# Stores through GpSimd's queue as single packets, and two tokens dealt to other engines

## The chip, the cores and the metric

The kernel runs on one core of a Trainium2 chip. The time is the device time of one execution in microseconds, as the median of several runs; the profile is one execution recorded by the hardware profiler. Its span, from the first to the last instruction, is a little shorter than the device time.

## What is computed

Each of 8 x 256 tokens has a row of 512 numbers and 8 gate weights, one per expert. The weights of a token are divided by their sum, and the row is written out eight times, each time multiplied by one of the eight normalised weights:

```
gate_weights = gate_weights / (np.sum(gate_weights, axis=-1, keepdims=True) + 1e-8)
output = x[:, :, None, :] * gate_weights[:, :, :, None]
```

All is float32. The inputs hold 4.26 MB, the output 33.55 MB: one multiplication per number written, and eight times as much written as read.

## The kernel before

The 2048 tokens are laid over 128 partitions, 16 tokens to a partition, so that what lies in one partition is contiguous in the output too. "Token j" below means the j-th token of every partition, so one step over j makes 128 x 8 x 512 numbers, 16 KB in each partition.

The inputs come in by four loads. The gates and the first two tokens (`HEAD`) are issued ahead of the barrier at the program's entry, from SyncE's and ScalarE's queue; tokens 2 to 12 (the body) and 13 to 15 follow on SyncE's queue (L72, L75). Lines 80 to 83 normalise all gates at once on VectorE.

The output is built in `ring`, which has ten slots of one token each. The list `CHUNKS` has five entries (first token, number of tokens, first slot): stores one to five write 2, 3, 3, 4 and 4 tokens. Stores four and five use slots again: tokens 8 and 9 take the slots 0 and 1 of store one, tokens 10 and 11 the slots 2 and 3 of store two, tokens 12 and 13 the slots 6 and 7 of store three; tokens 14 and 15 take the slots 8 and 9, which are new. A token that takes a used slot can't be computed before that slot's store has landed.

There are two ways to compute a token. `scale_one` makes one of its eight parts, on ScalarE (L90, an ACTIVATE) or on VectorE (L92, a TENSOR_SCALAR). `scale_token` makes all eight in one VectorE instruction (L95, a TENSOR_TENSOR). Before the change tokens 0, 1 and 3 are shared between both engines; token 2 and the first tokens of stores three, four and five (5, 8 and 12) are ScalarE's; all others, tokens 4 and 9 among them, are VectorE's by L95. The framework puts the instructions of each engine into an order of its own planning and adds the waits on semaphores; the order that results on VectorE for L95 is 4, 6, 7, 9, two tokens of the new slots, 10, 11, 13.

The stores are issued at L120, all on SyncE's queue, one after the other. Store one has an added dependency on the body load, so that it doesn't run among the loads. At the end (L157 of the launch) SyncE waits for all DMAs, and a barrier ends the program. GpSimd does nothing but set four constants at the start.

Of the kernel before, what the change touches and what calls it, by code (L numbers as in the profile page):

```python
# [1 line left out]

# [4 lines left out]

SLOTS = 10
HEAD = 2
TAIL = 13  # L10
CHUNKS = ((0, 2, 0), (2, 3, 2), (5, 3, 5), (8, 4, 0), (12, 4, 6))


def issue_before_entry_barrier(nc, loads):
    names = [bi.ins.name for bi in loads]

    def move(nc):
        blocks = nc.main_func.blocks
        entry = blocks[0].instructions
        moved = []  # L20
        for block in blocks[1:]:
            for ins in list(block.instructions):
                if ins.name in names:
                    block.instructions.remove(ins)
                    moved.append(ins)
        assert sorted(i.name for i in moved) == sorted(names)
        for ins in moved:
            at = next(k for k, other in enumerate(entry) if other.engine == ins.engine)
            entry.insert(at, ins)

    nc.at_finalize(move)


@with_exitstack
def kernel(
    ctx: ExitStack,
    tc: tile.TileContext,
    x: bass.AP,
    gate_weights: bass.AP,
    out: bass.AP,  # L40
):
    nc = tc.nc
    P = 128

    B, S, D = x.shape
    E = gate_weights.shape[-1]
    J = B * S // P

    fp32 = mybir.dt.float32
    mult = mybir.AluOpType.mult  # L50

    x_v = x.flatten_outer_dims().rearrange("(p j) d -> p j d", p=P)
    g_v = gate_weights.flatten_outer_dims().rearrange("(p j) e -> p j e", p=P)
    out_v = out.rearrange("b s e d -> (b s) e d").rearrange(
        "(p j) e d -> p j e d", p=P
    )

    pool = ctx.enter_context(tc.tile_pool(name="pool", bufs=1))

    g_all = pool.tile([P, J, E], fp32)  # L60
    x_all = pool.tile([P, J, D], fp32)
    ring = pool.tile([P, SLOTS, E, D], fp32)
    gsum = pool.tile([P, J, 1], fp32)
    gn = pool.tile([P, J, E], fp32)
    warm = pool.tile([P, 1], fp32)

    first_loads = [
        nc.sync.dma_start(out=g_all, in_=g_v),
        nc.scalar.dma_start(out=x_all[:, 0:HEAD, :], in_=x_v[:, 0:HEAD, :]),
    ]  # L70
    issue_before_entry_barrier(nc, first_loads)
    body_load = nc.sync.dma_start(  # L72
        out=x_all[:, HEAD:TAIL, :], in_=x_v[:, HEAD:TAIL, :]
    )
    nc.sync.dma_start(out=x_all[:, TAIL:J, :], in_=x_v[:, TAIL:J, :])  # L75

    nc.vector.memset(warm, 0.0)  # L77
    nc.scalar.copy(out=warm, in_=warm)  # L78

    nc.vector.reduce_sum(out=gsum, in_=g_all, axis=mybir.AxisListType.X)  # L80
    nc.vector.tensor_scalar_add(out=gsum, in0=gsum, scalar1=1e-8)  # L81
    nc.vector.reciprocal(out=gsum, in_=gsum)  # L82
    nc.vector.tensor_tensor(  # L83
        out=gn, in0=g_all, in1=gsum.to_broadcast([P, J, E]), op=mult
    )

    def scale_one(engine, j, e, slot):
        o_ap, s_ap = ring[:, slot, e, :], gn[:, j, e : e + 1]
        if engine is nc.scalar:
            nc.scalar.mul(out=o_ap, in_=x_all[:, j, :], mul=s_ap)  # L90
        else:
            nc.vector.tensor_scalar_mul(out=o_ap, in0=x_all[:, j, :], scalar1=s_ap)  # L92

    def scale_token(j, slot):
        nc.vector.tensor_tensor(  # L95
            out=ring[:, slot, :, :],
            in0=x_all[:, j : j + 1, :].to_broadcast([P, E, D]),
            in1=gn[:, j, :].unsqueeze(2).to_broadcast([P, E, D]),
            op=mult,
        )  # L100

    for j0, m, s0 in CHUNKS:
        for i in range(m):
            j, slot = j0 + i, s0 + i
            if j < 2:
                for e in range(E):
                    on_act = e < 3
                    scale_one(nc.scalar if on_act else nc.vector, j, e, slot)
            elif j == 2:
                for e in range(E):  # L110
                    scale_one(nc.scalar, j, e, slot)
            elif j == 3:
                for e in range(E):
                    scale_one(nc.scalar if e < 2 else nc.vector, j, e, slot)
            elif i == 0:
                for e in range(E):
                    scale_one(nc.scalar, j, e, slot)
            else:
                scale_token(j, slot)
        store = nc.sync.dma_start(  # L120
            out=out_v[:, j0 : j0 + m, :, :], in_=ring[:, s0 : s0 + m, :, :]
        )
        if j0 == 0:
            tc.add_manual_dep(
                store.ins,
                body_load.ins.name,
                mybir.DependencyInfo(
                    mybir.DependencyClass.Sync, mybir.DependencyReason.DATA
                ),
                reason="no store among the loads",  # L130
            )


# [1 line left out]
_INS = ['x', 'gate_weights']  # L135
_OUTS = [((8, 256, 8, 512), 'float32')]


# [23 lines left out]
```

## Time and profile before

The time before is 92.58 us, the median of 3 runs (92.5 to 92.65). The profiled span is 90.7 us.

| what | value | how to read it |
|---|---|---|
| DMA | 37.81 MB, 417 GB/s over the span | all 16 DMA engines of the core together |
| VectorE busy | 46.7 us of 90.7 | 9 TENSOR_TENSOR of 4420 ns, 16 TENSOR_SCALAR of 482 ns |
| ScalarE busy | 26.4 us | 40 ACTIVATE of 708 ns; overlapping, so eight take 5.0 us |
| GpSimd busy | 0.2 us | four MEMSETs |
| SyncE's final wait for DMA | 33.1 us | from the fifth store's issue to its landing |

In the profile, "SPq L120" is the issue of a store by SyncE's sequencer; the time to landing is counted from there to the moment at which its semaphore is complete. "A <- B" in the list of waits says that A waited for B, with the sum, the number of times and the longest.

### The profile page before, as it was taken

To read this page: it belongs to the slowest core of one execution; us is meant where nothing else is said; L and a number is where in the kernel's file an instruction comes from. 1 tells how busy PE (TensorE), PEld (TensorE's weight loads), DVE (VectorE), ACT (ScalarE), POOL (GpSimd) and SP (SyncE) were. 2 spreads that over 40 slices of the span, in tenths; PEclk is the share of its full clock that TensorE was granted. 3 is DMA by queue.
4 is the path that set the end of the run, shared out by engine and by line. 5 is a ranking of instruction groups with operands and counts; after the bars stand their busy time and mean duration, and the time that the engine had idled before them with its cause. 6 is when DMAs were issued, how large, how long until landed. Compare 5 with 4: busy or idle time off the path is not lost.

```text
span 90.7 us, 140 instructions
## 1 busy us (share of the span) xinstructions
DVE 46.7 (52%) x30; ACT 26.4 (29%) x42; POOL 0.2 (0%) x4
## 2 busy tenths in 40 slices
DVE  0795399999999999999990495000000000000000
ACT  5393399997990000000000497000000000000000
POOL 0000000000000000000000000000000000000000
DMA  4998999999898889888988999999999982999990
GB/s 110 468 467 378 383 536 463 463 390 419 347 694 347 347 347 694 347 347 347 694 347 347 463 463 463 463 463 463 463 463 463 463 347 116 463 463 463 463 463 0
DMA packets 1296, 37.81 MB, mean 417 GB/s; under 512 B 144, under 2 KB 272, under 8 KB 528
## 3 DMA queue, kind: packets, MB, share of 16 engines
q1 hardware_dynamic: 1152, 37.29, 95.5%
q10 hardware_dynamic: 144, 0.52, 1.6%
HBM read 4.26 MB, written 33.55 MB: 417 GB/s over the span
## 4 chain that ended last, share of the span: by engine, by line
DMA 38%; DVE 17%; ACT 5%; ACTq 1%; issue 0%; SPq 0%
DMA out_dram<-ring 28%; DVE ring L95 14%; DMA x_all<-in_x_dram 11%; ACT ring L90 5%; DVE ring L92 3%; ACTq L157 1%; ACTq L90 0%; SPq L120 0%
## 5 line engine op out<-in xcount | busy, mean ns | idle before, releaser
L95 DVE TENSOR_TENSOR ring<-x_all,gn 128x4096 f32<-128x4096 f32 x9 | 39.2, 4420 | 3.5 <-DMA out_dram<-ring 3.5
L90 ACT ACTIVATE ring<-x_all,gn 128x512 f32<-128x512 f32 x40 | 24.9, 708 | 28.8 <-DMA out_dram<-ring 24.5
L92 DVE TENSOR_SCALAR ring<-x_all,gn 128x512 f32<-128x512 f32 x16 | 6.5, 482 | 2.8 <-DMA x_all<-in_x_dram 2.8
L78 ACT ACT_TABLE_LOAD x1 | 1.3, 1283 | 0.9 <-PEq L146 0.9
L80 DVE TENSOR_REDUCE gsum<-g_all 128x16 f32<-128x128 f32 x1 | 0.3, 286 | 1.6 <-DMA g_all<-in_gate_weights_dram 1.6
L77 DVE MEMSET warm<- 128x1 f32 x1 | 0.1, 59 | 1.0 <-PEq L146 1.0
L83 DVE TENSOR_TENSOR gn<-g_all,gsum 128x128 f32<-128x128 f32 x1 | 0.3, 291 | 0.0
L82 DVE RECIPROCAL gsum<-gsum 128x16 f32<-128x16 f32 x1 | 0.3, 252 | 0.0
L78 ACT COPY warm<-warm 128x1 f32<-128x1 f32 x1 | 0.2, 191 | 0.0
L81 DVE TENSOR_SCALAR gsum<-gsum 128x16 f32<-128x16 f32 x1 | 0.2, 176 | 0.0
L146 POOL MEMSET const-bfloat16-1.0<- 128x1 bf16 x1 | 0.1, 102 | 0.0
L146 POOL MEMSET const-uint8-127<- 128x1 uint8 x1 | 0.1, 102 | 0.0
L146 POOL MEMSET const-float32-0.0<- 128x1 f32 x1 | 0.1, 99 | 0.2 <-issue 0.2
L146 POOL MEMSET const-float32-1.0<- 128x1 f32 x1 | 0.1, 99 | 0.0
## 6 DMA issues: line engine op xcount, KB each, us to landing
out_dram<-ring SPq DMA_DIRECT2D x2, 6144.0 KB, 22.1
out_dram<-ring SPq DMA_DIRECT2D x1, 4096.0 KB, 11.5
x_all<-in_x_dram SPq DMA_DIRECT2D x1, 2816.0 KB, 9.6
x_all<-in_x_dram SPq DMA_DIRECT2D x1, 768.0 KB, 11.1
x_all<-in_x_dram ACTq DMA_DIRECT2D x1, 512.0 KB, 3.7
g_all<-in_gate_weights_dram SPq DMA_DIRECT2D x1, 64.0 KB, 2.6
out_dram<-ring SPq DMA_DIRECT2D x2, 28.1
```

What stands on the lines that cost most here:

```text
L77: nc.vector.memset(warm, 0.0)
L78: nc.scalar.copy(out=warm, in_=warm)
L80: nc.vector.reduce_sum(out=gsum, in_=g_all, axis=mybir.AxisListType.X)
L81: nc.vector.tensor_scalar_add(out=gsum, in0=gsum, scalar1=1e-8)
L82: nc.vector.reciprocal(out=gsum, in_=gsum)
L83: nc.vector.tensor_tensor(out=gn, in0=g_all, in1=gsum.to_broadcast([P, J, E]), op=mult)
L90: nc.scalar.mul(out=o_ap, in_=x_all[:, j, :], mul=s_ap)
L92: nc.vector.tensor_scalar_mul(out=o_ap, in0=x_all[:, j, :], scalar1=s_ap)
L95: nc.vector.tensor_tensor(out=ring[:, slot, :, :], in0=x_all[:, j : j + 1, :].to_broadcast([P, E, D]), in1=gn[:, j, :].unsqueeze(2).to_bro ...
L146: nc = _bacc.Bacc("TRN2", target_bir_lowering=False, num_devices=1)
L157: with _tile.TileContext(nc) as tc:
```

## The change

The first store stays on SyncE's queue. Stores two to five are issued by GpSimd instead, whose queue holds nothing else. The flag `single_packet` asks that all of a store's descriptors on one DMA engine form one packet.

Besides, token 4, the last of store two, is made by eight TENSOR_SCALARs of VectorE (L92) in place of one TENSOR_TENSOR (L95); and token 9, the second of store four, goes from VectorE to eight ACTIVATEs of ScalarE (L90). Both are there to let stores two and four be issued earlier.

```diff
+SOFT_FROM = 2
 CHUNKS = ((0, 2, 0), (2, 3, 2), (5, 3, 5), (8, 4, 0), (12, 4, 6))
...
-            elif i == 0:
+            elif j == 4:
+                for e in range(E):
+                    scale_one(nc.vector, j, e, slot)
+            elif i == 0 or j == 9:
                 for e in range(E):
                     scale_one(nc.scalar, j, e, slot)
             else:
                 scale_token(j, slot)
-        store = nc.sync.dma_start(
-            out=out_v[:, j0 : j0 + m, :, :], in_=ring[:, s0 : s0 + m, :, :]
-        )
+        out_ap, in_ap = out_v[:, j0 : j0 + m, :, :], ring[:, s0 : s0 + m, :, :]
+        if j0 < SOFT_FROM:
+            store = nc.sync.dma_start(out=out_ap, in_=in_ap)
+        else:
+            nc.gpsimd.dma_start(out=out_ap, in_=in_ap, single_packet=True)
```

## The prediction

> **What bounds the kernel now.** I read the busy rows of the page first, then the DMA row, then the moments at which the five stores were issued and landed, and last the waits.
>
> ```profile
> span 90.7 us, 140 instructions
> DVE 46.7 (52%) x30; ACT 26.4 (29%) x42; POOL 0.2 (0%) x4
> DMA  4998999999898889888988999999999982999990
> DMA packets 1296, 37.81 MB, mean 417 GB/s; under 512 B 144, under 2 KB 272, under 8 KB 528
> q1 hardware_dynamic: 1152, 37.29, 95.5%
> ```
>
> No compute engine is busy for much more than half of the span, and the DMA row is 8 or 9 in nearly every slice from the second on (the lone 2 stands beside an 8 and is how whole 2.4 us packets fall into 2.27 us slices). One queue holds the 16 engines for 95.5% of the span. The next question is whether the stores ever run out of queued work.
>
> ```profile
> 10.60 45.91 SPq L120 DMA_DIRECT2D out_dram<-ring  x5
> 17.41 0.34 SPq L120 DMA_DIRECT2D out_dram<-ring  x1
> 26.08 0.33 SPq L120 DMA_DIRECT2D out_dram<-ring  x1
> 47.76 0.33 SPq L120 DMA_DIRECT2D out_dram<-ring  x1
> 56.18 0.33 SPq L120 DMA_DIRECT2D out_dram<-ring  x1
> ```
>
> These are the issues (start, length) of stores one to five; the times to landing of that line are 11.5, 19.1, 25.0, 22.7 and 33.6 us. Sums: they land at 22.1, 36.5, 51.1, 70.5 and 89.8. The distances are 14.4, 14.6, 19.4 and 19.3 us for 6.29, 6.29, 8.39 and 8.39 MB: 437, 431, 432 and 435 GB/s, with no hole at any boundary. Each store is issued long before its predecessor lands: ahead by 4.7, 10.4, 3.3 and 14.3 us. That margin is what the change can use up.
>
> ```profile
> ACT ring L90 <- DMA out_dram<-ring: 24.5, 2, 24.0
> DVE ring L95 <- DMA out_dram<-ring: 3.5, 1, 3.5
> SPq L157 <- DMA out_dram<-ring: 33.1, 1, 33.1
> ```
>
> The compute engines wait for the stores to free ring slots, and the end of the program waits 33.1 us for the last store. So the time is the head (first bytes at 1.0 us, the loads, store one behind them), then 67.7 us of stores two to five at 434 GB/s, then about 0.9 us from the last landing to the end of the span. The profile's chain turns to DVE before the third store, because a slot there was released late; with a full DMA row and 10.4 us of margin that part bounds nothing.
>
> **What the Trainium skill says.** "DMA: Bandwidth & Descriptors", section "Issuing engines are not separate DMA queues": a DMA issued from GpSimd runs on the same 16 engines as one from SyncE, so a new queue brings no bandwidth. The trace of before agrees as far as it goes: its two queues (q1 and q10) together never pass the rate of one. Same page, "Queues, rings and completion order": an engine takes turns between queues packet by packet. Here a later store shares the engines with store one. In the records of before, two body-load packets of 22,528 B on q1 took 1202 and 1180 ns where 836 is usual, a delay of two whole 4096 B packets (159 ns each) of q10 and a little more; an engine thus seems to stay with a queue for more than one record. "SBUF — State Buffer", "Who interferes with whom": descriptors for GpSimd's DMAs are written through a port pair that VectorE can lock; `tensor_scalar` in its two-port modes locks it, `tensor_tensor` takes only the read interface and is inferred not to stop descriptors. No GpSimd DMA is in the trace of before, so it can't say.
>
> **The change part by part.**
> *Token 4 from one `TENSOR_TENSOR` to eight `TENSOR_SCALAR`.* Removed: 4420 ns. Added: 8 at the pace of the six before it (2.47 us for six, 0.41 each), 3.3 us. VectorE then ends token 4 at 12.92 + 3.3 = 16.2 instead of 17.3. ScalarE's share of store two (tokens 2 and 3, ten instructions at 11.14/18 = 0.62 us from 10.53) ends at 16.7. So store two becomes ready at 16.7 instead of 17.4, and ScalarE is then what it waits for: 0.7 us more margin. These two-port instructions end before GpSimd can start on its first store, so they can't lock it.
> *Token 9 from VectorE to ScalarE.* VectorE loses 4.42 us between tokens 7 and the next; ScalarE gains 8 x 0.62 = 5.0 us right after token 8 (22.15 to 27.16), done at 32.2 in a stretch in which it waits 24.0 us. Tokens 6 and 7 follow token 4: done at 20.6 and 25.0, so store three is ready at 25.0 instead of 26.0. The two tokens that use fresh slots end at 33.7; tokens 10 and 11 need slots of store two, which lands at 36.5, so VectorE waits about 2.8 us there and ends at 36.5 + 2 x 4.4 = 45.3 instead of 47.7. Store four gains 2.4 us of margin. Tokens 12 and 13 wait for store three at 51.1 as now, 5.0 us: store five ready at 56.2, unchanged.
> *Issue on GpSimd.* Removed: four issues of 0.33 us on SyncE, which nobody waits for. Added: four waits and four descriptor jobs on GpSimd. Nothing else is queued there: its four MEMSETs end at 0.4 us. Price: on SyncE the first load's bytes flow 1.0 us after its issue; the skill's "Latency and other measured facts" gives about 1 us to the first byte for GpSimd and 0.6 for SyncE. I take 1.5 us, low end 1.0; as the high end the case in which descriptors wait for the `TENSOR_TENSOR` that is running, 4.4 + 1.0 = 5.4 us. Margins after the edits, to the landing of the store before: 22.1 - 16.7 = 5.4, 11.5, 51.1 - 45.3 = 5.8 and 14.3 us. Even the high end just fits. On the path: 0.
> *One packet per engine.* Each store has 8 rows per engine (128 over 16). In the packet records a 49,152 B row starts every 1812 ns and a 65,536 B row every 2414 ns. The slope is 602 ns per 16,384 B, 27.2 GB/s per engine, and what is left per row is about 6 ns. If one packet removes it for seven of eight rows: 4 x 7 x 6 = 0.17 us at most; if these gaps belong to rows and not to packets, 0. I take half, 0.08 us.
> *Two queues at once.* Store two is queued from about 18 us while store one has some 3.5 us left. Total bytes are the same; only the order could change.
> Sum: 0 - 0.08 us, so 92.5; I say 92.45, since the earlier readiness also leaves nothing to collide with.
>
> **The rivals.**
> *Faster: the row gaps do vanish, and the handover between stores with them.* 92.58 - 0.17, and with the 4 B record of 9 ns at each store's end some 0.2: 92.35. For it: nothing but the row gaps can still be saved, and they are there. Against it: it is hardly more than the bound of 0.2%.
> *Slower: the software queue runs a little under the hardware queue's rate.* The engines must fetch their descriptors from the memory that GpSimd wrote. "SBUF — State Buffer", "The DMA setup-cost knee", has 425 GB/s for 16 MiB where here 434 is measured. 29.36 MB at 425 take 69.1 us instead of 67.7: +1.4, 94.0 as the far end, 93.2 in the middle. Against it: only eight rows of 48 or 64 KB per engine and store, with time to fetch each next one.
> *Slower: descriptors starved.* If back-to-back `TENSOR_TENSOR`s lock GpSimd until VectorE first pauses (33.7 us), the stream stops from 22.1 to 34.7: +12.6, 105. If the lock passes between two of them, 16.7 + 5.4 = 22.1, nothing lost. For it only the shared port; against it the section above.
> *Slower: store two overtakes store one.* If an engine changes queues after every row of store one, the single packet (14.5 us) cuts in at about 19 us, with two rows of 1.2 us left; one follows at 34, the other behind store three at about 50. Tokens 8 and 9 wait for those slots, ScalarE then needs 10.0 us, and with 1.5 for the issue the queue is empty for about 11 us: 104. Against it: the records of two queues above. With only one row left it lands at about 35 and costs nothing (35 + 10 = 45, as VectorE).
>
> **How the numbers follow.** No change within 0.2% (92.39 to 92.77): 0.36, and the forecast lies in it. Faster: 0.34, of which most is 92.2 to 92.39 and a tenth of all lies further down, for fixed costs outside the span (92.58 - 90.7 = 1.9 us) that I can't see. Slower by a little (a lower rate, a late first descriptor): 0.18, at 92.8 to 94.0. Starved: 0.06. Overtaken: 0.06. The range runs from 91.9 to 94.0: it leaves out the last two cases and a few of a hundred at the low end. Faster 0.34, same 0.36, slower 0.30.
>
> **What would show it.** Right: the DMA row still 8 to 9 through to the end; landings of stores still 14.5 and 19.4 us apart; VectorE waiting some 3 us for the second store, and the fourth issue at about 45; the last wait still the longest. The packet term shows in those distances: shorter by 0.04 us each if the gaps go, longer by 0.3 to 0.4 at 425 GB/s. Starvation would show as a 0 in the DMA row after 22 us with GpSimd's issue long done or stretched; overtaking as a first store that lands after the second, ScalarE's token 8 late, and a hole near 52 us. The prediction is wrong if any wait of GpSimd lies behind something I don't see, if its first store costs over 5.4 us, or if the end of the program has to wait for GpSimd beyond the last landing.

## The result and the profile after

The changed kernel takes 93.85 us (median of 4 runs, 93.59 to 94.09) where the kernel before takes 92.62 (4 runs, 92.5 to 92.78) beside it: 1.0132 times as long, interval 1.0100 to 1.0163. Executions more than 1.5% above the fastest of their kernel are left out of all ratios and intervals, and kept in the medians. Two later comparisons on other chips gave 1.0076 (1.0047 to 1.0105) and 1.0090 (1.0055 to 1.0126). So the change makes the kernel slower, by 0.7 to 1.2 us.

The page of the changed kernel: span, the DMA row in 40 slices, GpSimd's queue (packets, MB, share of the 16 engines), and the body load's time from issue to landing.

```profile
span 91.9 us, 153 instructions
DMA  4999899699799779977997999999999998589990
q0 software_dynamic: 576, 29.36, 74.2%
x_all<-in_x_dram SPq DMA_DIRECT2D x1, 2816.0 KB, 10.4
```

The DMA row has no hole after store one begins: GpSimd's queue is fed in time. But the body load lands after 10.4 us, where the profile of before has 9.6 (the line below), and everything behind it is late by as much. That alone is 0.8 of the 1.2 us between these two spans, and it lies ahead of the first instruction that the change touches.

```profile
x_all<-in_x_dram SPq DMA_DIRECT2D x1, 2816.0 KB, 9.6
```

The order of time, the lines of GpSimd's issues and of VectorE's two tokens of store four (start, length; idle time ahead of it and its releaser):

```profile
17.89 0.67 POOL L128 DMA_DIRECT2D out_dram<-ring  x1 [17.45 <-ACT ring L91]
26.22 0.53 POOL L128 DMA_DIRECT2D out_dram<-ring  x1 [7.67 <-ACT ring L91]
37.45 8.76 DVE L96 TENSOR_TENSOR ring<-x_all,gn 128x4096 f32<-128x4096 f32 x2 [3.14 <-DMA out_dram<-ring]
46.77 0.53 POOL L128 DMA_DIRECT2D out_dram<-ring  x1 [20.02 <-DVE ring L96]
57.34 0.53 POOL L128 DMA_DIRECT2D out_dram<-ring  x1 [10.04 <-ACT ring L91]
```

Less the 0.8 us of the late head, the plan of the compute engines is as predicted: VectorE waits 3.1 us for store two (2.8 predicted), and store four is ready at 45.4 (45.3). Store one lands at 22.85; the landings that follow, at 37.4, 51.95, 71.4 and 90.8, are 14.5, 14.6, 19.5 and 19.3 us apart: within 0.1 us of before. What is new must be sought in tenths of a microsecond: in the head, in those distances, at the end, and outside the span.

Which wait ended last changed in one point. SyncE's waits in the changed kernel:

```profile
SPq L163 <- DMA out_dram<-ring: 79.0, 1, 79.0
```

Before, this line had 33.1 us: SyncE worked off the first waits of its final list while the stores ran, and then waited for store five. Now it waits from 11.8 us on, so the very first wait of the list is the one for the last store, and all others are worked off behind it.

### The profile page after: what moved, and what is told of

Same layout as the page of the kernel before. It is cut to its first block, busy times and chain, and to the rows that moved or that the text cites. A ratio compares the mean times of both kernels' runs of the same rounds, so it can differ in the third digit from the quotient of the medians.

```text
span 91.9 us, 153 instructions
## 1 busy us (share of the span) xinstructions
DVE 41.3 (45%) x36; ACT 31.3 (34%) x50; POOL 2.5 (3%) x8
## 4 chain that ended last, share of the span: by engine, by line
DMA 52%; DVE 5%; ACT 3%; issue 1%; POOLq 1%; SPq 0%; DVEq 0%; ACTq 0%
DMA out_dram<-ring 40%; DMA x_all<-in_x_dram 11%; DVE ring L96 5%; ACT ring L91 3%; POOLq L163 1%; SPq L126 0%; DVEq L96 0%; POOLq L128 0%; ACTq L91 0%
## 5 line engine op out<-in xcount | busy, mean ns | idle before, releaser
L91 ACT ACTIVATE ring<-x_all,gn 128x512 f32<-128x512 f32 x48 | 29.8, 708 | 24.8 <-DMA out_dram<-ring 19.7
L96 DVE TENSOR_TENSOR ring<-x_all,gn 128x4096 f32<-128x4096 f32 x7 | 30.6, 4420 | 9.0 <-DMA out_dram<-ring 9.0
L93 DVE TENSOR_SCALAR ring<-x_all,gn 128x512 f32<-128x512 f32 x24 | 9.7, 481 | 4.0 <-DMA x_all<-in_x_dram 4.0
L128 POOL DMA_DIRECT2D out_dram<-ring x4 | 2.3, 565 | 55.2 <-ACT ring L91 35.2
L78 DVE MEMSET warm<- 128x1 f32 x1 | 0.1, 59 | 1.0 <-PEq L152 1.0
## 6 DMA issues: line engine op xcount, KB each, us to landing
x_all<-in_x_dram SPq DMA_DIRECT2D x1, 2816.0 KB, 10.4
x_all<-in_x_dram SPq DMA_DIRECT2D x1, 768.0 KB, 11.8
```

Source lines behind the costliest of these rows:

```text
L96: nc.vector.tensor_tensor(out=ring[:, slot, :, :], in0=x_all[:, j : j + 1, :].to_broadcast([P, E, D]), in1=gn[:, j, :].unsqueeze(2).to_bro ...
L128: nc.gpsimd.dma_start(out=out_ap, in_=in_ap, single_packet=True)
```

## The experiments

Each ran with the kernel before beside it on the same chip. "Outside the span" is the device time less the recorded span, as a mean over a kernel's runs.

**The parts alone.** Dealing alone (in `after`: `SOFT_FROM = 16`, so all stores stay on SyncE):

> Tokens 4 and 9 dealt as in the changed kernel, but all five stores on SyncE's queue. Theory A (the loss belongs to GpSimd's queue): as before, 92.6 within 0.2, the fourth store ready some 2 us earlier and nothing gained from it. Theory B (the loss belongs to the new dealing, which moves what VectorE and ScalarE do beside the loads): 93.8, with the body load landing at 11.3 us instead of 10.5.

GpSimd's queue alone:

```diff
-            elif j == 4:
-                for e in range(E):
-                    scale_one(nc.vector, j, e, slot)
-            elif i == 0 or j == 9:
+            elif i == 0:
```

> Stores two to five on GpSimd's queue as single packets, tokens 4 and 9 where they were before. Theory A: 93.8 to 94.0, as the changed kernel, since the margins of 3 us and more still hide the issue. Theory B: 92.6. Should the longer issue on GpSimd eat the margin of the fourth store (3.3 us before), a hole would show near 51 us and the time would be above 94.

The last store alone through GpSimd (`SOFT_FROM = 12`):

> Dealt as in the changed kernel, only the fifth store through GpSimd as a single packet. If the loss is one of each store (slower packets), a quarter to a third of it: 92.9 to 93.0. If it is a fixed price of a program that uses GpSimd's queue at all (head and end), 93.6 to 93.9. If it is the head of the chip run alone and not the change, 92.6.

And the changed kernel again:

> The changed kernel once more, for a second profile and a comparison on the chip of the runs beside it. 93.8. If the late body load of its first profile (11.3 us, one packet of 1949 ns) was chance, it is back at about 10.5 here and the time at 93; if it belongs to the change, it is late again.

Measured: dealing alone 92.87, ratio 1.0032 (1.0006 to 1.0058); queue alone 93.62, 1.0071 (1.0035 to 1.0107); last store alone 93.07, 1.0033 (1.0005 to 1.0060); the changed kernel 93.46, 1.0076. The kernel before: 92.67. Neither theory holds alone: both parts seem to cost something, though the first by an amount near what can be told. Single runs of most kernels, of before too, spread from their best by over 1 us.

The queue-alone kernel also gives the price of an issue on GpSimd, because there the margin of store four is as small as before. Its issue of store four:

```profile
48.48 0.53 POOL L125 DMA_DIRECT2D out_dram<-ring  x1 [21.13 <-DVE ring L96]
```

The wait ahead of it ends at 47.96, and the first record of store four is at 50.77, 2.8 us later. Store three's last rows end between 50.70 and 51.08, and, in order of time, the rows of store four start 0.06 us behind them on average and at most 0.12, where in the profiles of before and of the changed kernel it is 0.003. A margin of 3.1 us from the ready moment is thus just used up by GpSimd; the new dealing is needed to hide it. The 2.8 us are an upper value for the issue alone, since the engines were at work on store three until then.

**Presence, framing, and the kernel before as a control.**

> The kernel before, unchanged, run as if it were an experiment: its ratio to itself shows what a comparison can tell, and it gives a second profile of before. Theory C (the head is chance: in every kernel one engine's load packet may stall by 0.5 to 2 us, and store one waits for the slowest engine): body load's end scatters here too, between 10.2 and 12 us, ratio 1.00 within 0.3%. Rival (the head is slower only in the changed kernels): body load again at 10.5 and the time at 92.5.

Without the flag:

```diff
-            nc.gpsimd.dma_start(out=out_ap, in_=in_ap, single_packet=True)
+            nc.gpsimd.dma_start(out=out_ap, in_=in_ap)
```

> The changed kernel without single_packet. If the packets' framing costs (or saves) time, the distance of the last stores' landings changes from 19.4 us and the total moves against 93.5; if framing is without effect, as I now think, 93.4 to 93.6 as the changed kernel, store packets of 1820 and 2425 ns. If store two shares the engines with the rest of store one, row by row, store one lands late, near 25 us, and nothing else moves.

The flag on SyncE's queue, in the kernel before (`single_packet=j0 > 0` at L120):

> The kernel before with single_packet on stores two to five, still on SyncE's queue. If the 6 ns between rows go with one packet per engine: 92.4, packets pitched at 1806 and 2408 ns. If they belong to rows: 92.6, pitches 1812 and 2414. If the framing itself is what makes the changed kernel slower: above 93.

A tiny DMA on GpSimd's queue in the kernel before (`nc.gpsimd.dma_start(out=spare, in_=warm)` after L78):

> The kernel before, plus one DMA of 4 bytes in each partition (SBUF to SBUF) on GpSimd's queue near the start; all stores on SyncE's. If the loss is a fixed price of GpSimd's queue being used at all (end of the program, 0.2 us from the last packet to the end, and the head): 92.8 to 93.3. If it grows with what goes through the queue: 92.6 to 92.7, with the end at 1.2 us as before.

Measured: before against itself 92.64, ratio 0.9983 (0.9962 to 1.0004); without the flag 93.17, 1.0061 (1.0034 to 1.0089); the flag on SyncE 92.69, 0.9990 (0.9959 to 1.0021); the tiny DMA 92.80, 1.0006 (0.9980 to 1.0032). So framing brings nothing on either queue. GpSimd's queue costs little by its presence, at most 0.3 us by this interval; the profile of the tiny DMA has 1.31 us from the last packet to the end of the span where before has 1.19 to 1.22. (This DMA, issued at 2.69 us among the loads, has its first record at 6.60, 3.9 us later.) The control shows how far a comparison can be trusted: 0.2%. Its body load landed after 9.7 us, those of the others between 9.5 and 10.8, and after 11.7 in the second profile of the changed kernel. Dealing alone had 10.8 with all its stores on SyncE, and the changed kernel without the flag 9.6: a late head needs no store on GpSimd, and such a store doesn't always bring it. In the records of such a late head there are one or two 22,528 B rows of 1.4 to 2.4 us in place of 0.84, and store one waits for the slowest engine.

**The stores without the scatter.** To see tenths, three kernels leave out the loads and all arithmetic:

```diff
+    for slot in range(4):
+        nc.vector.memset(ring[:, slot, :, :], 1.0)
...
+        out_ap, in_ap = out_v[:, j0 : j0 + m, :, :], ring[:, 0:m, :, :]
```

> Stores alone: the loads and all arithmetic are left out, the ring is set to 1.0 and the same five stores go out, all on SyncE's queue. No load can stall, so runs should agree within 0.2 us; the output is 1.0 everywhere. About 77.5 us of stores behind a head of 4 to 6 us: 83 to 86.

> The same stores alone (no loads, no arithmetic, the output 1.0 everywhere), stores two to five through GpSimd as single packets. Against the same on SyncE: +0.3 to +0.45 us, if it is the end (0.2) and the four slow rows (0.15). If GpSimd's queue has a lower rate: +1 and more, in all rows. If the greater loss of the changed kernel comes from the loads: less than 0.2. Store two is issued while store one is in full flow: if a single packet cuts in between rows of store one, store one lands after store two.

> As the run before it (no loads, no arithmetic, the output 1.0 everywhere), without single_packet. If framing is without effect: the same time within 0.1 us and the same order of rows. If engines take turns row by row without the flag, rows of stores one and two alternate here and not with the flag.

Measured: 91.02 on SyncE, 91.32 through GpSimd as single packets, 91.32 without the flag, each within 0.02 us over six runs. The pages of the first two, with store one's line:

```profile
span 89.2 us, 53 instructions
q1 hardware_dynamic: 720, 33.55, 87.2%
out_dram<-ring SPq DMA_DIRECT2D x1, 4096.0 KB, 11.2
```

```profile
span 89.6 us, 53 instructions
q0 software_dynamic: 576, 29.36, 76.0%
out_dram<-ring SPq DMA_DIRECT2D x1, 4096.0 KB, 13.2
```

GpSimd's queue costs 0.30 us, fifteen times the scatter, and the flag 0.00. (My 83 to 86 us left out that the four memsets come one by one, so that store one starts at 9.4 us; the differences don't hang on it.) The packet records show where: the mean over the 16 engines of each engine's n-th row, in ns.

```
                         rows of store one (32,768 B)                 store two (49,152 B)
all on SyncE             1219 1250 1218 1231 1228 1222 1214 1232      1834 1820 1820 1820 ...
GpSimd, single packets   1219 1248 1218 1220 1250 1295 1223 1219      1914 1832 1821 1820 ...
GpSimd, no flag          1219 1248 1218 1220 1248 1299 1223 1220      1914 1833 1822 1820 ...
```

GpSimd issues at 13.99 to 15.18 and 18.25 to 19.30. The fifth and sixth row of store one (15.2 to 17.8 us) and the first two of store two (20.2 to 24) follow these issues, and together they are 187 ns longer than on SyncE; all later rows are equal within 3 ns. The rate of the queue is thus not lower; rows that are under way after an issue take longer. By what means, no record shows. The other 0.1 us is at the end: from the last packet to the end of the span 1.27 us instead of 1.15.

Store two does not overtake store one here. It is issued with half of store one still to go, yet store one's rows end at 20.32 (on SyncE 20.23), in their usual order, flag or no flag. But store two's first row comes at 20.24, some 6.2 us after the issue, when store one has no row left, so that rows of the two never compete. Only store one's landing is 2.0 us later, 13.2 for 11.2: the 4 B records that complete its semaphore come at 22.06 to 22.25, behind the first row of store two.

The last store back on SyncE (`if j0 < SOFT_FROM or j0 == 12`):

> The changed kernel with the fifth store back on SyncE's queue, stores two to four on GpSimd's. The theory has two terms: (1) at the end, SyncE's list of final waits begins with the semaphore of the last GpSimd store, so that the waits for long finished DMAs are worked off behind it, 0.06 us each; (2) rows in transfer while GpSimd issues a store take some 40 ns longer. Taking the last store away should bring back the end (from the last packet to the end 1.2 us instead of 1.43) and one of four such rows: 92.8 to 93.0 where the changed kernel has 93.5. If the loss lies in stores two to four, 93.3 to 93.5.

92.98, ratio 1.0038 (1.0014 to 1.0062): between the kernel before and the changed one. Its waits on SyncE:

```profile
SPq L163 <- DMA out_dram<-ring: 33.0, 2, 25.9
```

The last wait of the list is again the one that ends last, and from the last packet to the end it takes 1.18 us, as in the kernel before (1.19 to 1.22). With the last store alone on GpSimd one wait is left behind the one for it, and the end takes 1.27. So it is the order of the waits that costs, and the end's term is shown.

In these two kernels stores four and five are on different queues, and rows of both are under way together. For the last store alone on GpSimd, the DMA queues between 62 and 77 us, and the times to landing of stores four (SyncE) and five (GpSimd):

```profile
q1 hardware_dynamic: 48, 3.15, 48.5%
q0 software_dynamic: 48, 3.15, 48.5%
out_dram<-ring SPq DMA_DIRECT2D x1, 34.7
out_dram<-ring POOLq DMA_DIRECT2D x1, 33.4
```

The queues share the engines row by row. In the packet records each engine changes the queue after every 65,536 B row, from store five's first row (62.8 us, 6.2 after its issue) until store four is through, although store five goes as a single packet. Store four lands at 80.4 us, and with the queues exchanged, in the kernel above, at 82.7, where it lands at 70.4 before. That costs nothing, because no token waits for store four's slots. In the changed kernel only stores one and two are on different queues, and store one's last rows end 4.2 to 4.6 us after store two's issue (17.89; 22.09 to 22.50): too early for store two's rows to come between.

**All together on one chip.** By now the measured 0.30 us stood against a loss of 0.7 to 1.2.

> The changed kernel a third time, on one chip with the three kernels beside it. The stores alone cost 0.30 us more through GpSimd's queue. Theory C (the rest is the head, which is chance and the same for all kernels): best runs at 92.75 to 92.95, median 93.0 to 93.2, ratio 1.004 to 1.006. Rival (the changed kernel's head is slower in most runs): best runs above 93.1, ratio 1.007 and more.

> The changed kernel without single_packet, again. Theory C: as the changed kernel beside it within 0.1 us, best and median. Rival (the flag matters where loads and arithmetic are in the kernel, though not for the stores alone): 93.15 here and 93.5 or more there.

> The new dealing with all stores on SyncE's queue, again. Theory C: 92.6 to 92.7, as the kernel before, so that its 92.87 of the first time was the head's chance. Rival (the new dealing costs 0.2 to 0.3 us by itself): 92.85 again, best runs at 92.55 where the kernel before has 92.35.

> The kernel before, as an experiment again: ratio 1.000 within 0.2%, best runs 92.4, some runs above 93.3.

Measured: the changed kernel 93.28, ratio 1.0090; without the flag 93.34, 1.0100 (1.0067 to 1.0133); dealing alone 92.89, 1.0033 (1.0019 to 1.0047); before 92.56, 1.0001 (0.9978 to 1.0023). The theory of mere chance falls: the dealing alone costs 0.3 us again, and its best run is 92.65 to 92.36. Yet the spans of dealing alone and of before are the same (medians 90.9 and 90.8). The difference lies outside the span:

| kernels | token 9 on ScalarE | stores on GpSimd | outside the span, us |
|---|---|---|---|
| before, in five comparisons | no | no | 1.78 to 1.79 |
| flag on SyncE; tiny DMA; queue alone | no | none; tiny; 4 | 1.79; 1.78; 1.78 |
| dealing alone, twice | yes | no | 1.98, 2.01 |
| last store; all but the last | yes | 1; 3 | 2.00; 2.01 |
| without the flag, twice | yes | 4 | 1.98, 2.04 |
| changed kernel, three times | yes | 4 | 2.02, 1.99, 2.05 |

The trace goes on for a little after the last instruction. DMA between 91 and 95 us of the changed kernel's first profile (q14 fetches program), and of the kernel before in the last comparison:

```profile
DMA packets 1, 0.01 MB, mean 2 GB/s; under 512 B 0, under 2 KB 0, under 8 KB 0
...
q14 instruction: 1, 0.01, 0.8%
```

```profile
DMA packets 0, 0.00 MB, mean 0 GB/s; under 512 B 0, under 2 KB 0, under 8 KB 0
```

All kernels with token 9 on ScalarE fetch one more piece of 8192 B of program some 1.75 us after their last recorded instruction; none of the others does. Which half of the dealing is it?

> All stores on SyncE's queue, token 4 by eight TENSOR_SCALARs (seven instructions more on VectorE), token 9 where it was. Theory: the dealing costs 0.2 us after the span, where in all kernels with eight more ACTIVATEs on ScalarE one more 8 KB piece of program is fetched, so here there is no such fetch, 1.79 us of the time lie outside the span, and the time is 92.55 as before. Rival: VectorE's longer program, or any, is the cause: the fetch is there, 2.0 us outside, 92.8.

> All stores on SyncE's queue, token 9 on ScalarE (eight ACTIVATEs more there, one instruction less on VectorE), token 4 where it was. Theory (ScalarE's program is what crosses a piece's end): one fetch of 8 KB some 1.8 us after the last instruction, 2.0 us outside the span, 92.8. Rival (VectorE's): no fetch, 1.79 outside, 92.55.

Token 4 alone (seven more instructions on VectorE): 1.80 us outside the span (22 runs), and no fetch. Token 9 alone (eight more on ScalarE): 2.01 us outside (22 runs), and the fetch; the same window of the latter:

```profile
DMA packets 1, 0.01 MB, mean 2 GB/s; under 512 B 0, under 2 KB 0, under 8 KB 0
...
q14 instruction: 1, 0.01, 0.7%
```

So it is ScalarE's longer program. (VectorE's is longer by six instructions with the dealing alone and shorter by one with token 9 alone, and both have the fetch; its length doesn't decide.) The device times of these two don't tell it (92.79 and 92.81, ratios 0.9997 and 0.9999, each within 0.2%), because spans scatter by as much: medians 91.0 and 90.8 there. That the fetch itself takes the 0.2 us is inferred from the two always coming together; what reads that piece of program after the end the trace doesn't show.

**The account.** The third comparison has both kernels with a like head (body load landed after 9.5 and 9.7 us), the changed one first:

```profile
span 90.9 us, 153 instructions
x_all<-in_x_dram SPq DMA_DIRECT2D x1, 2816.0 KB, 9.5
```

```profile
span 90.8 us, 140 instructions
x_all<-in_x_dram SPq DMA_DIRECT2D x1, 2816.0 KB, 9.7
```

Term by term, from their records: rows of stores two to five, 16 x 1822.0 + 16 x 2426.0 ns against 16 x 1818.4 + 16 x 2420.6, +0.14 us. Some 0.1 of it lies about the issues again: in stores two to four the slow rows are the fourth (1846), the seventh (1846) and the fourth (2462), in flight some 1.5 to 3 us after GpSimd's issues and 29 to 38 ns longer than their neighbours. In the kernel before, the rows after SyncE's issues are longer too, but by 8 to 12 ns. The rest is spread over the 65,536 B rows, up to 7 ns each, and stays open. Nor does every issue show: that of store two left store one's rows as they were here (1217 and 1215), where the first profile has one of 1268. The end, from the last packet to the end of the span: 1.46 against 1.20, +0.26; 0.20 of it are the four final waits that are left behind the last landing in place of one, as the records of SyncE show (start and length in ns):

```
changed   10932 78914 the last store's semaphore   89888 28   89950 28   90014 28   90076 27   90141 DRAIN
before    56960 32979 the last store's semaphore   89973 28   90038 DRAIN
```

The remaining 0.06 lie behind that DRAIN: 0.79 us to the end of the span against 0.73. With the tiny DMA it is 0.80, so a single DMA on GpSimd's queue is enough for it.

Outside the span: 2.05 against 1.79, +0.26. Together +0.66; the medians of the runs that the ratios count differ by 0.73 here and by 0.73 in the second comparison, which leaves 0.1 for the head. In the first comparison (1.23) some 0.6 us are not the change's fixed price; in its profile 0.8 us lie in the body load. That the head is worse by chance, and not a little worse in the changed kernel, is likely but not shown: with 4 to 22 runs a kernel I can't tell 0.1 us there.

## Why the prediction was wrong

What bounds the kernel, the plan of the engines and the margins were right: the stream of stores stays full, store four was ready where I put it, VectorE waits those three microseconds, and no wait of GpSimd reaches the path. The rivals of starved descriptors and of overtaking did not come true, the second not for the reason set against it. I took two load rows, delayed by two small packets each, as a sign that an engine stays with a queue for more than one record. With 65,536 B rows it changes after every one, flag and all; store two escaped because its rows came only when store one had none left.

Four points were not.

- "Issue on GpSimd ... On the path: 0" is the step that failed. I asked only whether the issue is hidden by the store before, and it is; its cost is what it does to others. Rows in flight after its issues are slower, 0.1 to 0.19 us in all; as the last store's semaphore now stands first in SyncE's final list, 0.2 us of waits for long finished DMAs follow the last landing; and 0.06 us more pass behind that list. I had named that list ("the end of the program has to wait for GpSimd") as a thing that could make me wrong, and not looked at its order: before, four of its five waits were done or under way when store five landed.
- "Token 9 from VectorE to ScalarE" was costed in engine time alone. It is free there; eight more instructions cost 0.2 us outside the span, which I had only set down as fixed costs that I couldn't see, and counted on the fast side.
- The saving by single packets, 0.08 us and at most 0.17, is 0.00: 91.32 with and without the flag, 92.69 with it on SyncE. The 6 ns belong to rows.
- The price of an issue, from the ready moment to the first bytes, was nearer to 2.8 us, its upper value in the kernel with the queue alone, than to 1.5; the tiny DMA took 3.9 among the loads. All margins still held it, but without the new dealing store four's would just have failed.

"The software queue runs a little under the hardware queue's rate" came near in size (93.2 in the middle) by luck, for a reason that the runs refute: away from the issues its 49,152 B rows take 1817 to 1820 ns, as on SyncE, and in the kernels without loads all rows do within 3 ns.

The statements of the Trainium skill that the prediction rested on were borne out in the main. "DMA: Bandwidth & Descriptors", "Issuing engines are not separate DMA queues": no bandwidth came with the queue, and the issue time that it saves on SyncE was worth nothing. The same page, "Queues, rings and completion order": an engine takes turns between queues packet by packet. Where rows of two queues met, the turn was one row of 65,536 B, and the flag did not make a store's eight rows on an engine one turn; no run shows such a meeting without the flag. "SBUF — State Buffer", "Who interferes with whom": two-input `tensor_tensor` did not stop descriptors; store two was issued in the middle of one (16.89 to 21.3) and nothing ran dry.

## What to carry to other kernels

When the transfers already fill the span, a change of the issuing queue has little to win; look at what it adds after the last landing (the order of the final waits) and outside the span (device time less span, and program fetches beyond the last instruction), where no engine row shows it. Before explaining a loss under 1%, run the old kernel against itself and build a kernel with only the disputed part: here that took the spread from over 1 us to 0.02 and showed a price of 0.30 us at once. And a margin that hides the issue says nothing on what the issue does to transfers under way. With stores on two queues, count on the earlier one landing late when rows of both are under way: here by 10 to 12 us.

## What had not been expected of the hardware

- A piece of 8192 B of program is fetched some 1.75 us after the end of the span when ScalarE has 50 busy instructions in place of 42, and the time outside the span is then 2.0 us and not 1.79.
- With no loads in the kernel, device times repeat within 0.02 us; with them, one engine's load row can take 1.4 to 2.4 us in place of 0.84, and a store that waits for the whole load takes all of it on.
- Two stores on different queues share each engine row by row, 65,536 B at a turn, with `single_packet` too: store four then lands at 80.4 or 82.7 us in place of 70.4.
- The 49,152 B row of a late-head profile takes 1820 ns on nearly every engine, that of an early one 1815. In the profiles of the kernels that compute it goes with the head; the kernels without loads have 1820. Why was not found.
